# A hybrid attention layer: the softmax-times-values products as one operation per four key blocks

## The chip, the cores and the metric

The kernel runs on one core of one Trainium2 chip. The metric is the device time of one execution in microseconds. One execution was also recorded by the hardware profiler; all durations below come from it.

## The reference

One decoder layer with 1024 tokens and a model width of 1024. A normalised and modulated input is projected once; its columns belong to four groups of four heads with 64 values each: A differential, B forgetting, C stick-breaking and D sparse attention. The outputs are concatenated, projected and added to the input; a gated MLP with a short convolution follows. The change is in the last product of each attention (weights `w`, `p` or `a` times values), which the four groups share in form:

```python
def block(i):                      # 128 query rows
    ...
    p = jax.nn.softmax(s, axis=-1)
    return jnp.einsum('bhqk,bhkd->bhqd', p.astype(v.dtype), v)
```

A takes `w = p0 - lam * p1` of two softmaxes, C takes `a = exp(log_beta + tail)`. D has three such products; the selected and the window branch (at most five key blocks per query block) go through the code of the change.

## The kernel before, in words

**A program with its own scheduler.** The kernel does not issue instructions as it goes. Each helper (`mm`, `mm2`, `tr`, `copy`, `act`, `dma` and others, lines 410 to 497) records an operation through `Program.op` (line 174) with a planned length on each engine that could do it, the tiles it reads and those it writes. At the end `schedule` (line 224) plays the program through: for each engine it takes the oldest recorded operation that is ready, where ready means that its predecessors are done in the plan (plus the delays of the table `WAITS`) and that its new tiles have a slot. `issue` (line 377) then emits the instructions in that order, so the order in each engine's queue is fixed before the run; on the chip the queues go in that order and wait on semaphores. All instructions carry line 392, so groups are told apart by their tiles. One operation may hold several instructions (`mm2` holds two); nothing is placed between them.

**Slots.** The table at lines 538 to 552 gives each class of tile a quota, a group and a phase. Group `h` has 28 slots of 128 x 512 floats; a class of a later phase gets a slot only beyond the quotas of the earlier phases that are not used up. In phase 2 it holds `qst` (queries, 4), `pt` (transposed weights, 3), `ot` (output before it is transposed back, 2) and `on` (output, 2). The projections' `wr`, `wh`, `nt` and `hl` (19 in all) are phase 1. PSUM group `q` has 8 banks: four `S` (scores), two `T` (transposes), one `O` (attention output) and one `pP` (projections).

**Attention.** `attn_A`, `attn_C`, `attn_D` and `attn_B` (lines 963, 1159, 1097, 1244) run in this order. Each takes two heads at a time and query blocks of 128 rows in groups of four; block i sees n/128 = i + 1 key blocks (the window branch of D at most five). For each query block the scores go to `S`, the row minima are taken on VectorE, the exponentials on ScalarE, and the weights land in tiles `P`. Between these operations the program order mixes other matrix work: projections into `pP` beside A, C and D (`side`), the first half of the output projection beside B (`out_AC`).

**The product** is `pv_pair` (line 890), called once for each query block and head pair. For every two key blocks it transposes four 128 x 128 pieces of `P` (two blocks, two heads) into one `T` bank, copies the bank to a `pt` tile on ScalarE or VectorE (line 902), and records one `mm2` (line 419) for each key block: two matmuls that use the left and right 64 columns of TensorE for the two heads and accumulate in `O`. A matmul on 32-bit data is two records in the trace, so an `mm2` is four. `back` (line 907) copies `O` to `ot` and transposes it once the four query blocks are done. By the code there are 16 calls each in A, B and C and 32 in D, with 348 `mm2` in all; ten calls each have one, two, three and four key blocks, sixteen have five, and eight each have six, seven and eight.

Of the kernel before, what the change touches and what calls it, by code (L numbers as in the profile page):

```python
# [27 lines left out]
STEP = 1.3  # L28
EARLY = 2
DCUT = (2, 3, 3, 3)  # L30

CA_Q, CA_K, CA_V = 0, 256, 512
CB_Q, CB_K, CB_V, CB_F = 768, 1024, 1280, 1536
# [110 lines left out]
class Program:  # L144
# [274 lines left out]
    def mm2(self, outs, lhsTs, rhss, start, stop):  # L419
# [6 lines left out]
        d = max(d, 1.26 * self._mm_use(lhsTs[0], rhss[0]))  # L426
        self.op([("PE", d, f)], list(lhsTs) + list(rhss), list(outs)).share = 2.0 * self._mm_use(lhsTs[0], rhss[0]) / d

    def tr(self, out, in_, ident):
        self.op([("PE", 109.0, self._call("tensor", "transpose", (out, in_, ident), {}))], [in_, ident], [out])  # L430

# [69 lines left out]
def layer_kernel(ctx: ExitStack, tc, x, c, rel_bias, ada_w, ada_b, norm_mix_g, norm_ffn_g, w_in, w_out,  # L501
# [4 lines left out]
    K = Program(tc)  # L506
    NB, NH = 33, 28
    pool = lambda n, b, **k: ctx.enter_context(tc.tile_pool(name=n, bufs=b, **k))
    cp, bp, hp, sp = pool("cp", 1), pool("bp", 1), pool("hp", 1), pool("sp", 1)
# [7 lines left out]
    def const(shape, dt=F32, name="const"):  # L517
        ncls[0] += 1
        k = f"c{ncls[0]}_{name}"
        K.klass(k, 1, "c", 0)  # L520
        return K.tile(k, shape, dt, name)
# [12 lines left out]
    for name, quota, group, phase in (  # L534

# [7 lines left out]

# [6 lines left out]

# [2 lines left out]
        K.klass(name, quota, group, phase)  # L553
# [4 lines left out]
    def hb(cls, dt=F32):  # L558
        return K.tile(cls, (128, 512), dt)

    def ps1(cls):
        return K.tile(cls, (128, 512))


    ident = const([128, 128], name="ident")
# [324 lines left out]
    def pv_pair(P, n, vfn, dst):  # L890

        nb = n // 128
        for g0 in range(0, nb, 2):
            g1 = min(nb, g0 + 2)
            t = ps1("T")
            for j in range(g0, g1):
                for u in range(2):
                    c = 2 * (j - g0) + u
                    K.tr(t[:, c * 128:(c + 1) * 128], P[u][:, j * 128:(j + 1) * 128], ident)
            pt = hb("pt")  # L900
            w = (g1 - g0) * 256
            K.copy(pt[:, :w], t[:, :w])
            for j in range(g0, g1):
                c = 2 * (j - g0) * 128
                K.mm2([dst[0:64], dst[64:128]], vfn(j), [pt[:, c:c + 128], pt[:, c + 128:c + 256]], j == 0, j == nb - 1)

    def back(o):

# [54 lines left out]
    def attn_A(p, st):  # L963
        st, bias = st
        for i0 in (0, 4):
# [3 lines left out]
            for i in range(i0, i0 + 4):  # L969
                n = (i + 1) * 128  # L970
                Ps = []
                for u in range(2):
                    P, L = two("P", n), []
                    for m, s in enumerate(scores([[(qs[2 * u + m], st[2 * u + m][1])] for m in range(2)], i, 0, n)):
                        c = 2 * (i - i0) + u
                        l = [l0s[:, c + v:c + v + 1] for v in (0, 8)] if m == 0 else [small("l1", 1) for v in s]
                        exps(P[m], s, rows_min(s, n, bias[u]), l)
                        if len(s) > 1:
                            K.tt(l[0], l[0], l[1], OP.add)
                        L.append(l[0])  # L980
                    cf = small("cf", 1)
                    K.recip(cf, L[1])
                    K.ts(cf, cf, L[0], nlam, OP.mult, OP.mult)
                    K.stt(P[0], P[1], cf, P[0], OP.mult, OP.add)
                    Ps.append(P[0])
                pv_pair(Ps, n, VA.pair(p), o[:, (i - i0) * 128:(i - i0 + 1) * 128])
                yield i * 1.3 + STEP
# [109 lines left out]
    def attn_D(p, st):  # L1097
        qf, bias, biasC = st
        for i0 in (0, 4):
# [31 lines left out]
            for br in (1, 2):  # L1131
                o = ps1("O")
                l = small("dl", 16)
                for i in range(i0, i0 + 4):
                    k0 = 0 if br == 1 else max(0, i - 4) * 128
                    n = (i + 1) * 128 - k0
                    P = two("P", n)
                    for u, s in enumerate(scores([[(q[u], D_k[br - 1, 0]), (q[u], D_k[br - 1, 1])] for u in range(2)], i, k0, n)):
                        c = 2 * (i - i0) + u
                        exps(P[u], s, rows_min(s, n, bias[u], wmask if (br == 2 and i >= 4) else None),  # L1140
                             [l[:, c + v:c + v + 1] for v in (0, 8)])
                    pv_pair(P, n, lambda j: [VD[0][:, k0 // 128 + j, br - 1, :]] * 2, o[:, (i - i0) * 128:(i - i0 + 1) * 128])
                    yield (n / 128 - 1) * 1.3 + STEP
                f = small("df", 8)
                if i0:
                    K.tt(l[:, :8], l[:, :8], l[:, 8:], OP.add)
                K.recip(f, l[:, :8])
                K.tt(f.split(2), gates[:, i0:i0 + 4, 4 * br + 2 * p:4 * br + 2 * p + 2], f.split(2), OP.mult)
                t = on_tile()
                K.tt(t, back(o), f.bc(64), OP.mult)  # L1150
                K.tt(on, on, t, OP.add, ("POOL", "DVE"))
# [7 lines left out]
    def attn_C(p, st):  # L1159
        qf, k = st  # L1160
        for i0 in (0, 4):
            q = qf(i0)
            o = ps1("O")
            for i in range(i0, i0 + 4):
                n = (i + 1) * 128
                W = two("P", n)
                for u, z in enumerate(scores([[(q[u], k[u][0]), (q[u], k[u][1])] for u in range(2)], i, 0, n)):
                    w = W[u]
                    cs = [slice(512 * v, 512 * v + t.n) for v, t in enumerate(z)]
                    for c, t in zip(cs, z):  # L1170
                        K.act(w[:, c], t, AF.Abs)
                    K.act(w, w, AF.Exp, scale=-1.0)
                    K.act(w, w, AF.Ln, bias=1.0)
                    for c, t in zip(cs, z):
                        K.stt(w[:, c], t, 0.0, w[:, c], OP.max, OP.add)
                    K.select(w[:, n - 128:n], w[:, n - 128:n], [[-1, 128]], OP.is_gt, 0.0, 0, 1)
                    K.scan(w[:, ::-1], w[:, ::-1])
                    for c, t in zip(cs, z):
                        K.tt(w[:, c], t, w[:, c], OP.subtract)
                    K.select(w[:, n - 128:n], w[:, n - 128:n], [[-1, 128]], OP.is_gt, -BIG, 0, 1)  # L1180
                    K.act(w, w, AF.Exp)
                pv_pair(W, n, VC.pair(p), o[:, (i - i0) * 128:(i - i0 + 1) * 128])
                yield i * 1.3 + STEP
            t = on_tile()
            K.copy(t, back(o))
            o_out(2, i0, p, t)
# [471 lines left out]
    def down_mul(n, ps=None):  # L1658
# [3 lines left out]
        q0 = 0  # L1662
        for c in DCUT:
            ops = {}
# [88 lines left out]
```

## Time and profile before

| | before |
|---|---|
| median of 3 runs | 1491.72 us |
| lowest and highest run | 1485.66 and 1492.05 us |
| the profiled execution's own time | 1490.82 us |
| its span, first to last instruction | 1489.1 us |
| mean granted clock of TensorE, share of full | 0.978 |
| attention with its side work | from about 214 to 790 us of the span |

How to read the profile: PE is TensorE's matmuls, PEld its weight loads, which overlap the matmuls; DVE is VectorE, ACT ScalarE, POOL GpSimd. A group like `O<-pt,V` names the written tile and the read ones; `128*64 128x128` after it is the part of the array that is used (rows by columns) and the moving operand. Matmuls are pipelined, so the time a run of matmuls holds PE is read from its first start to the start of what follows, and the last one's own duration overlaps with what follows.

### The profile page before, as it was taken

Reading aid. Unit: us, or ns where it says so; the run is one execution under the profiler, and the core shown is the slowest. Engines: PE = TensorE matmul, PEld = TensorE weight load, DVE = VectorE, ACT = ScalarE, POOL = GpSimd, SP = SyncE. Lnnn points to the kernel's source line nnn. Section 1 sums busy time; section 2 is a strip of 40 time slices with the busy share of each in tenths; the row PEclk is TensorE's granted clock in tenths of the full one; section 3 lists DMA queues with packets and bytes.
Section 4 is the critical chain, followed back from the end, with each engine's and each line's share of the span. In section 5 each row is a group of like instructions: output and inputs, shape, how many; then the busy total and the mean of one; then the engine's idle time right before and its main releaser. Section 6 shows DMA issues by size and latency. Waiting matters only on the chain.

```text
span 1489.1 us, 24140 instructions
## 1 busy us (share of the span) xinstructions
PE 1389.8 (93%) x8573; PEld 1174.1 (79%) x8573; DVE 1120.2 (75%) x2382; ACT 703.0 (47%) x1529; POOL 217.3 (15%) x249
## 2 busy tenths in 40 slices
PE   3999999999799998999999789999999999999998
PEld 2878888888687886777877568888888888888886
DVE  7966668999779986775475886666666665898777
ACT  2531245657678655663364644334444443453342
POOL 3543310223323355100000000000000000000000
PEclk9999999999899998999999899999999999999999
DMA  9679463535431423145534322222222224963675
GB/s 353 209 213 319 134 171 93 170 91 155 114 76 49 133 92 98 41 105 162 161 105 155 113 86 86 80 83 85 85 85 80 84 85 169 370 238 99 226 248 170
DMA packets 169963, 211.24 MB, mean 142 GB/s; under 512 B 25517, under 2 KB 112214, under 8 KB 169842
## 3 DMA queue, kind: packets, MB, share of 16 engines
q1 hardware_dynamic: 168338, 208.52, 44.9%
q0 software_dynamic: 1504, 1.17, 0.5%
q8 instruction: 67, 1.10, 0.3%
q14 instruction: 54, 0.44, 0.1%
HBM read 165.30 MB, written 47.89 MB: 143 GB/s over the span
## 4 chain that ended last, share of the span: by engine, by line
PE 71%; DVE 12%; ACT 2%; issue 1%; DMA 1%; POOL 0%; SPq 0%; DVEq 0%; POOLq 0%; ACTq 0%
PE up L392 28%; PE dn L392 14%; PE pP L392 10%; PE T L392 7%; PE O L392 5%; PE S L392 4%; DVE P L392 4%; PE op L392 3%; ACT P L392 1%; DVE S L392 1%; DVE m L392 1%; DVE pt L392 1%; DVE nt L392 1%; DVE gB L392 1%; DVE hl L392 1%
## 5 line engine op out<-in xcount | busy, mean ns | idle before, releaser
L392 PE MATMUL up<-gB,fw 128*128 128x512 f32 x1320 | 303.6, 389 | 5.7 <-DVE fw L392 2.9
L392 PEld LDWEIGHTS up<-gB,fw 128*128 128x128 f32 x1320 | 247.5, 188 | 58.2 <-DVE fw L392 3.3
L392 PE MATMUL dn<-ds 128*128 128x512 f32 x924 | 209.9, 389 | 0.2 <-DVE ds L392 0.2
L392 PEld LDWEIGHTS dn<-ds 128*128 128x128 f32 x924 | 173.4, 188 | 36.6 <-DVE ds L392 0.6
L392 PE MATMUL pP<-wh,hT 128*128 128x256 f32 x1344 | 198.3, 292 | 3.4 <-DVE nt L392 1.3
L392 PEld LDWEIGHTS pP<-wh,hT 128*128 128x128 f32 x1344 | 178.7, 195 | 9.3 <-DVE nt L392 2.1
L392 ACT ACTIVATE P<-S,nm 128x512 f32<-128x512 f32 (+3 forms) x240 | 135.4, 571 | 81.9 <-DVE nm L392 63.6
L392 PE MATMUL S<-kst,qst 128*128 128x512 f32 (+2 forms) x480 | 134.0, 372 | 9.7 <-ACT P L392 5.7
L392 PE MATMUL up<-gA,fw 128*128 128x512 f32 x528 | 126.8, 395 | 7.6 <-DVE fw L392 7.6
L392 PE MATMUL T<-ident,P 128*128 128x128 f32 x696 | 113.1, 285 | 14.9 <-ACT P L392 8.9
L392 PEld LDWEIGHTS up<-gA,fw 128*128 128x128 f32 x528 | 99.8, 190 | 29.2 <-DVE fw L392 8.6
L392 PEld LDWEIGHTS T<-ident,P 128*128 128x128 f32 x696 | 79.8, 144 | 33.6 <-issue 15.1
L392 PEld LDWEIGHTS S<-kst,qst 128*128 128x128 f32 x480 | 79.1, 193 | 22.8 <-ACT P L392 9.0
L392 ACT COPY pt<-T 128x512 f32<-128x512 f32 (+1 forms) x106 | 56.5, 539 | 67.3 <-PE T L392 66.2
L392 DVE COPY pt<-T 128x512 f32<-128x512 f32 (+1 forms) x94 | 58.5, 627 | 38.6 <-PE T L392 36.1
L392 DVE TENSOR_REDUCE m<-S 128x1 f32<-128x512 f32 (+3 forms) x160 | 76.6, 488 | 7.5 <-PE S L392 6.7
L392 ACT CAST ds<-dg 128x512 fp32r<-128x512 f32 x82 | 48.2, 619 | 63.7 <-DVE dg L392 40.3
L392 DVE TENSOR_TENSOR fw<-fr,fw 128x512 fp32r<-128x512 f32 x110 | 75.1, 684 | 0.0
L392 ACT CAST fw<-fr 128x512 fp32r<-128x512 f32 x110 | 67.5, 614 | 9.6 <-DVE fw L392 9.5
L392 ACT ACTIVATE P<-P 128x256 f32<-128x256 f32 (+8 forms) x98 | 64.9, 690 | 11.5 <-POOL P L392 7.5
L392 PE MATMUL O<-pt,V 128*64 128x128 f32 x864 | 65.7, 287 | 4.2 <-DVE pt L392 2.3
L392 DVE SCALAR_TENSOR_TENSOR acc<-ada,cact,acc 128x512 f32<-128x512 f32 (+1 forms) x70 | 66.5, 950 | 3.1 <-DMA ada<-in_ada_w_dram 1.9
(295 smaller groups left out, 2323.2 us busy)
## 6 DMA issues: line engine op xcount, KB each, us to landing
dg<-d_g SPq DMA_DIRECT2D x99, 256.0 KB
fr<-in_ffn_w_up_dram SPq DMA_DIRECT2D x88, 256.0 KB
ada<-in_ada_w_dram SPq DMA_DIRECT2D x64, 256.0 KB
dg<-in_ffn_w_down_dram SPq DMA_DIRECT2D x55, 256.0 KB
d_g<-va SPq DMA_DIRECT2D x22, 512.0 KB
ada<-in_ada_w_dram SPq DMA_DIRECT2D x16, 512.0 KB
wr<-in_w_in_dram SPq DMA_DIRECT2D x32, 256.0 KB
x<-in_x_dram SPq DMA_DIRECT2D x8, 512.0 KB
```

Of the source, the lines that this page charges most:

```text
L392: return getattr(getattr(self.nc, eng), meth)(*a, **k)
```

## The change

A constant `PVB = 4` is added. `pv_pair` now goes over up to four key blocks at a time: it first records the transposes and copies of one or two `T` tiles, and then all products of these blocks and both heads as one operation `mms`, whose planned length is 0.5 x 1.03 of a matmul's use for each product plus 190 ns. The quota of `pt` goes from 3 to 4. `mm2` stays for another user.

```diff
+PVB = 4
...
+    def mms(self, prods):
+
+        fs = [self._call("tensor", "matmul", (o, a, b), dict(start=st, stop=sp)) for o, a, b, st, sp in prods]
+
+        def f():
+            return [g() for g in fs][-1]
+        d = len(prods) * 0.5 * 1.03 * self._mm_use(prods[0][1], prods[0][2]) + 190.0
+        u = len(prods) * self._mm_use(prods[0][1], prods[0][2])
+        self.op([("PE", d, f)], [x for p in prods for x in p[1:3]], [p[0] for p in prods]).share = u / d
...
-            ("qst", 4, "h", 2), ("pt", 3, "h", 2), ("ot", 2, "h", 2), ("on", 2, "h", 2),
+            ("qst", 4, "h", 2), ("pt", 4, "h", 2), ("ot", 2, "h", 2), ("on", 2, "h", 2),
...
-        for g0 in range(0, nb, 2):
-            g1 = min(nb, g0 + 2)
-            t = ps1("T")
-            for j in range(g0, g1):
-                for u in range(2):
-                    c = 2 * (j - g0) + u
-                    K.tr(t[:, c * 128:(c + 1) * 128], P[u][:, j * 128:(j + 1) * 128], ident)
-            pt = hb("pt")
-            w = (g1 - g0) * 256
-            K.copy(pt[:, :w], t[:, :w])
-            for j in range(g0, g1):
-                c = 2 * (j - g0) * 128
-                K.mm2([dst[0:64], dst[64:128]], vfn(j), [pt[:, c:c + 128], pt[:, c + 128:c + 256]], j == 0, j == nb - 1)
+        for h0 in range(0, nb, PVB):
+            h1 = min(nb, h0 + PVB)
+            pts = []
+            for g0 in range(h0, h1, 2):
+                g1 = min(h1, g0 + 2)
+                t = ps1("T")
+                for j in range(g0, g1):
+                    for u in range(2):
+                        c = 2 * (j - g0) + u
+                        K.tr(t[:, c * 128:(c + 1) * 128], P[u][:, j * 128:(j + 1) * 128], ident)
+                pt = hb("pt")
+                w = (g1 - g0) * 256
+                K.copy(pt[:, :w], t[:, :w])
+                pts += [pt[:, c:c + 128] for c in range(0, w, 128)]
+            K.mms([(dst[64 * u:64 * u + 64], vfn(j)[u], pts[2 * (j - h0) + u], j == 0, j == nb - 1)
+                   for j in range(h0, h1) for u in range(2)])
```

## Rows read from the trace of the kernel before

**Rows 1.** The page, part 1: busy us (share of the span) and instructions.

```profile
PE 1389.8 (93%) x8573; PEld 1174.1 (79%) x8573; DVE 1120.2 (75%) x2382; ACT 703.0 (47%) x1529; POOL 217.3 (15%) x249
```

**Rows 2.** Groups, 214 to 790 us, O matmuls: busy, mean ns | idle before <-releasers.

```profile
L392 PE MATMUL O<-pt,V 128*64 128x128 f32 x864 | 65.7, 287 | 4.2 <-DVE pt L392 2.3 <-ACT pt L392 1.7
...
L392 PE MATMUL O<-pt,VD 128*64 128x128 f32 x528 | 40.0, 288 | 0.1
```

**Rows 3.** Table of stretches: window, length, busy us by engine, clock, DMA, GB/s.

```profile
core 0: us, PE busy (x) PEld busy (x) DVE busy (x) ACT busy (x) POOL busy (x), PEclk, DMA share, GB/s
214.00:790.00 576.00, 532.76 (x4395) 452.15 (x4396) 454.67 (x1257) 339.40 (x882) 137.95 (x162) 0.97 0.39 111
214.00:290.00 76.00, 71.01 (x585) 62.20 (x585) 69.49 (x234) 46.37 (x143) 12.01 (x10) 0.98 0.47 134
290.00:375.00 85.00, 76.29 (x630) 67.53 (x630) 80.50 (x253) 55.67 (x165) 28.21 (x40) 0.97 0.48 127
375.00:523.00 148.00, 134.16 (x1197) 119.11 (x1196) 125.66 (x244) 104.03 (x209) 47.24 (x73) 0.96 0.34 95
523.00:600.00 77.00, 68.56 (x587) 56.09 (x585) 56.82 (x166) 41.90 (x111) 42.85 (x36) 0.93 0.33 97
600.00:690.00 90.00, 83.74 (x698) 68.21 (x699) 66.00 (x221) 51.22 (x153) 7.64 (x6) 0.96 0.27 75
690.00:790.00 100.00, 99.00 (x707) 79.01 (x706) 56.20 (x145) 40.22 (x108) 0.00 (x0) 1.00 0.48 150
```

**Rows 4.** Timeline of PE: start us, length us, what, records [idle before].

```profile
214.88 0.44 PE L392 MATMUL O<-pt,V 128*64 128x128 f32 x4 [0.42 <-DVE pt L392]
...
342.24 0.87 PE L392 MATMUL pP<-wh,hT 128*128 128x256 f32 x6
343.03 1.09 PE L392 MATMUL O<-pt,V 128*64 128x128 f32 x16
344.06 0.88 PE L392 MATMUL T<-ident,P 128*128 128x128 f32 x6
...
346.29 0.88 PE L392 MATMUL O<-pt,V 128*64 128x128 f32 x12
347.10 0.66 PE L392 MATMUL T<-ident,nt 128*128 128x128 f32 x4
...
352.91 2.66 PE L392 MATMUL pP<-wh,hT 128*128 128x256 f32 x20
355.41 0.82 PE L392 MATMUL T<-ident,P 128*128 128x128 f32 x6
...
357.90 1.09 PE L392 MATMUL T<-ident,P 128*128 128x128 f32 x8
358.75 0.94 PE L392 MATMUL S<-kst,qst 128*128 128x384 f32 x4
359.62 1.09 PE L392 MATMUL O<-pt,V 128*64 128x128 f32 x16
...
364.77 0.44 PE L392 MATMUL O<-pt,V 128*64 128x128 f32 x4
365.14 0.65 PE L392 MATMUL T<-ident,P 128*128 128x128 f32 x4
...
782.07 1.09 PE L392 MATMUL O<-pt,V 128*64 128x128 f32 x16
```

**Rows 5.** Timeline of PE from 641 us, a pair whose products run in two parts.

```profile
642.01 1.02 PE L392 MATMUL O<-pt,VD 128*64 128x128 f32 x8
642.97 1.31 PE L392 MATMUL T<-ident,P 128*128 128x128 f32 x10
644.03 0.48 PE L392 MATMUL S<-kst,qst 128*128 128x512 f32 x1
644.44 1.31 PE L392 MATMUL O<-pt,VD 128*64 128x128 f32 x20
```

**Rows 6.** Groups, 214 to 790 us, transposes and their copies (columns as in rows 2).

```profile
L392 PE MATMUL T<-ident,P 128*128 128x128 f32 x695 | 112.8, 285 | 14.9 <-ACT P L392 8.9 <-DVE P L392 2.5 <-DVE hl L392 1.7
...
L392 DVE COPY pt<-T 128x512 f32<-128x512 f32 (+1 forms) x94 | 58.5, 627 | 38.6 <-PE T L392 36.1 <-issue 1.8
L392 ACT COPY pt<-T 128x512 f32<-128x512 f32 (+1 forms) x106 | 56.5, 539 | 67.3 <-PE T L392 66.2
```

## The prediction

> **What bounds the kernel now.** I read the page first: TensorE (PE) is busy 93% of the span, VectorE (DVE) 75%, ScalarE (ACT) 47% [rows 1]. A shorter PE program could therefore shorten the whole. The weights-times-values products write the PSUM tile O; they run in a part of the span only, from 214.9 to 783 us [rows 2, 4]. So the second view is the table of stretches [rows 3]. In the 576 us from 214 to 790, PE is busy 532.8 and idle 43.2. The reader should see that DVE is nearly as full as PE in 290 to 375 (80.5 of 85 us) and in 375 to 523 (125.7 of 148), that PE's idle share is highest in 523 to 600 (8.4 of 77 us; the granted clock there is 0.93, a mean of mostly the 2.4 GHz level and partly the 1.2 GHz one), and that in 690 to 790 PE has almost no idle time (1.0 of 100). Third, the timeline of PE, which decides this case: it shows in which runs the O products stand in PE's queue [rows 4].
>
> **What the runs look like now.** By the code, 80 calls of pv_pair make 348 products of one key block for both heads. A record is half a matmul, so such a product is four records: 864 + 528 = 1392 records [rows 2]. The diff suggests short runs before, one for each transposed tile: 196 tiles, 196 runs of at most 8 records. The timeline shows something else. Going through PE's order from the first O row to the last [rows 4] and joining neighbours, I count 118 runs: 19 of 4 records, 32 of 8, 16 of 12, 40 of 16, 9 of 20 and 2 of 24. The scheduler takes the oldest ready instruction, and by the time PE is free for a pair's first product the second tile has mostly been copied too. So the run of four key blocks and both heads (16 records) is already the usual form.
>
> **Cost of a run.** From start to start in [rows 4]: the run of 4 records at 364.77 holds PE until 365.14, 0.37 us; 12 records from 346.29 to 347.10, 0.81; 16 from 343.03 to 344.06, 1.03. That is 0.055 us per record and 0.15 us fixed on leaving. On entering, six pP matmuls ahead of a run take 0.79 (342.24 to 343.03), while twenty take 2.50 (352.91 to 355.41), 0.75 for six: 0.04 more. I take 0.2 us per run. The busy time agrees: 1392 x 0.055 = 76 us, and 118 runs with the tail of a row (0.44 less 4 x 0.055, or 0.22) make 26; together 102 of the 105.7 us in [rows 2].
>
> **The change, part by part.**
> 1. *Fewer runs.* After it there are at most 120 operations of one run each: 40 pairs of one to four blocks with one, 40 pairs of five to eight with two. Neighbours can still merge, as the run of 20 at 644.44 did [rows 5]. Of the sixteen pairs with five blocks, five run in one piece now; I keep that (11 x 2 + 5 = 27), give the 24 longer pairs 48 and the short ones 40, which is 115, less the five merges across pairs that I count now: 110. So 118 becomes 110: 8 x 0.2 = 1.6 us less. The bounds: 120 runs, 0.4 us more; 80 runs, 38 x 0.2 = 7.6 us less. I take 1.6, because the order now already follows the same grouping in most pairs.
> 2. *A run waits for its second copy.* The first products could start after one tile; now the whole operation is placed after both. 16 pairs now begin with a run of two blocks and get the rest later, as at 642.01 and 644.44 [rows 5]. The price per pair lies between nothing and one copy, 0.63 us on DVE [rows 6]: 0 to 10 us. I take 0: what covers it is what stands in PE's queue between those two runs, 2.4 us from start to start filled with transposes and scores without idle. If that cover goes, the copy (0.6 us) is what is late. PE now waits for pt only 4.0 us in front of O in all [rows 2]. Behind a waiting run stand in PE's order the projections, scores and transposes of the next pair; for those exps on ACT and row minima on DVE wait.
> 3. *The fourth pt tile.* It adds no instruction and no transfer. The transposes (695 records), the 200 copies (94 on DVE and 106 on ACT) [rows 6] and every DMA stay. It lets the copies of blocks five to eight land while the first run still holds two tiles. It also takes a slot of the 28 that pt shares with qst, ot and on, so a result tile can come later. Both only move waits; 0, bounds in 4.
> 4. *Another order.* The planned lengths change. By the code one, two, three and four blocks were 269, 538, 806 and 1075 ns and become 410, 629, 849 and 1069; against the 0.37, 0.81 and 1.03 us of part one the new ones are even by 0.04, the old were short for short runs. So the scheduler will place the whole attention part somewhat differently, with the DMA issues on SP and the masks on POOL in that part as well. No row shows another order, so I bound it by stages [rows 3]: if the 576 us had the idle share of 214 to 290 (5.0 of 76, 6.6%), idle would be 38, 5 us less; with that of 523 to 600 (10.9%) it would be 63, 20 us more. I take 0, as the present total is nearer to the lower end, and keep both ends.
> 5. *pv_pair's other work* keeps its kind and count; the final output, out projection and the gated MLP from 790 us on are untouched.
>
> Sum: -1.6 us on the profiled execution's 1490.8 (span 1489.1 and 1.7 around it), so 1489.2. The median of the three runs, 1491.7, stands 0.9 above it: 1490.
>
> **A rule weighed.** The timeline shows 0.15 to 0.2 us lost at each run's ends. The Trainium skill, page TensorEngine Tiling (Array Packing), section Tiling Modes, says that changing the tiling mode drains TensorE, and O runs on 128 by 64 tiles between 128 by 128 work, so the trace agrees. Taken with the diff alone it would promise the gain of the first rival. The same page, section Performance Considerations, speaks against a gain: tiling does not speed the PSUM eviction, which may become the limit; by it the sum would be 0. Here the eviction is unchanged, 115 us on two engines [rows 6], and DVE's share bears that out in 290 to 523 but not after 690 [rows 3].
>
> **Rivals.**
> *A, face value: the runs fall by as many as the tiles suggest.* 196 - 120 = 76 runs less at 0.2 = 15 us: 1476. For it: the loss per run is plain, and PE is nearly full. Against it: the timeline has 118 runs, not 196. Only a merging to about 80 (-7.6) with less idle time besides would get near. Chance 0.08.
> *B, the pipeline closes up.* With the first run placed later and a tile more, the transposes of blocks five and six go in front of the first run, and their copies pass behind it. Now both groups of transposes follow that run (8 records at 357.90, the next run at 359.62) [rows 4]. It would take half of PE's idle in 375 to 600 (13.8 + 8.4 = 22.3 us): -11, and -1.6 from runs: 1478. For it: those pairs wait now. Against it: PE is filled by pP meanwhile, and DVE at 85% and more of 290 to 523 would be the next limit. Chance 0.16.
> *C, slower: the second copy is waited for.* In the stretch from 523 to 690 PE has little other work to lay in between, and the 16 pairs that start after one tile must wait for four more transposes (0.43 us: eight start at 357.90 and the next work at 358.75 [rows 4]) and a copy (0.63 us): 16 x 1.06 = 17 us, 1508 with the 0.9 above. It decides as soon as PE has less than about 1 us of other ready work at that point. For it: clock 0.93 and 11% idle there. Against it: 0.1 us of idle in front of those O records now [rows 2]. Chance 0.15.
> *The forecast, no change that can be told:* 0.61.
>
> **How the numbers follow.** About 0.5%, 7.5 us, is what a measurement of this kernel can tell from no change; its three runs spread over 6.4. A and B are faster by more, 0.24; the forecast is the same, 0.61; C is slower, 0.15. The range: below, the forecast's own ends (-1.6 - 5 - 4) and B give 1478; above, part 2's whole bound of 10 us gives 1500. A's and most of C's chance lie outside.
>
> **What would show it.** Right: the O runs number 105 to 120 with the 16-record run still the commonest; PE's busy time on O falls by about 2 us from 105.7; PE's idle from 214 to 790 stays within 38 to 50 us; DVE and ACT copies unchanged in sum. A would show fewer than 90 runs and O at 95 us. B would show transposes ahead of the first run in pairs of five to eight blocks, and less idle from 375 to 600. C would show PE waiting for pt in front of O for 10 us or more. The forecast is wrong if the idle moves by over 8 us either way, above all if the granted clock in 523 to 600 leaves 0.93, or if stages after 790 change, which nothing here touches.

## The result, and the profile after

The changed kernel takes 1479.67 us (median of five runs, 1476.49 to 1481.05) against 1491.72 before: ratio 0.9932, interval 0.991 to 0.9954, so 10 us less, with 7 to 13 as bounds (the two medians alone are 12 apart). The time lies inside the range of the prediction, but beyond the 0.5% that it called no change; that outcome had a chance of 0.24.

The profiled execution after took 1479.34 us with a span of 1477.6, 11.5 us less than the profiled one of before. The page after, part 1 (answers to [rows 1]):

```profile
PE 1382.1 (94%) x8573; PEld 1172.4 (79%) x8573; DVE 1119.3 (76%) x2380; ACT 700.1 (47%) x1525; POOL 228.4 (15%) x255
```

PE has the same number of records and 7.7 us less busy time. The O groups from 214 to 790 us (answers to [rows 2]), and the transposes and copies (to [rows 6]):

```profile
L393 PE MATMUL T<-ident,P 128*128 128x128 f32 x695 | 112.7, 284 | 12.7 <-ACT P L393 7.1 <-DVE P L393 3.5 <-ACT qk_y L393 0.8
...
L393 PE MATMUL O<-pt,V 128*64 128x128 f32 x864 | 64.7, 289 | 4.3 <-DVE pt L393 4.2
...
L393 DVE COPY pt<-T 128x512 f32<-128x512 f32 (+1 forms) x97 | 59.8, 624 | 29.0 <-PE T L393 27.9 <-issue 0.2 <-DMA kst<-d_bk 0.2
L393 ACT COPY pt<-T 128x512 f32<-128x512 f32 (+1 forms) x103 | 55.0, 540 | 59.6 <-PE T L393 56.6 <-PE S L393 1.8
...
L393 PE MATMUL O<-pt,VD 128*64 128x128 f32 x528 | 36.2, 280 | 0.0
```

O holds PE for 100.9 us in place of 105.7, the copies for 114.8 in place of 115.0, and PE waits for pt in front of O as long as before (4.2 us against 4.0). In PE's order I count 99 runs of O in place of 118: pairs of up to four blocks have one run each, 15 of 16 pairs with five blocks have one, and in D even six, seven and eight blocks join.

Where did the time go? The first and last starts of O by its value tile (VD is D's), before and after, date the stages:

```profile
L392 PE MATMUL O<-pt,V x864: 272/273/476, 214.9 to 782.9; 128*64 128x128 f32 x173
L392 PE MATMUL O<-pt,VD x528: 272/273/476, 523.5 to 673.3; 128*64 128x128 f32 x176
```

```profile
L393 PE MATMUL O<-pt,V x864: 272/273/477, 215.7 to 771.9; 128*64 128x128 f32 x173
L393 PE MATMUL O<-pt,VD x528: 272/273/477, 523.6 to 662.0; 128*64 128x128 f32 x176
```

A and C end where they ended: D's first product starts at 523.5 and 523.6 us. From the last O start to the end it is nearly equal too (706.2 and 705.7 us). In this pair of traces nearly the whole gain lies in D, whose products end 11.3 us earlier. The table of stretches for D's two head pairs, the first cut at the first O of the second pair and the second at the first O of B, before and after (columns as in [rows 3]):

```profile
523.50:615.60 92.10, 80.78 (x669) 66.44 (x668) 69.71 (x218) 52.34 (x146) 45.09 (x37) 0.93 0.31 90
615.60:675.40 59.80, 56.42 (x521) 46.13 (x520) 44.53 (x149) 35.46 (x103) 3.61 (x3) 0.97 0.26 66
```

```profile
523.60:605.80 82.20, 75.25 (x662) 64.43 (x661) 68.23 (x211) 53.09 (x149) 46.01 (x39) 0.95 0.34 101
605.80:664.10 58.30, 54.05 (x519) 45.45 (x519) 42.23 (x143) 35.40 (x103) 3.60 (x3) 0.98 0.27 68
```

The first pair of heads in D takes 82.2 us in place of 92.1: PE is busy 5.5 us less and idle 4.4 us less. Of the busy time there, O has 2.8 us less (18.21 against 21.04, in 17 runs in place of 26), and the projections pP have 1.7 us less, because ten of their records (79 against 89) now stand outside this pair. Before, PE had there a stretch in which it stood (timeline of PE before, and below it the table row of the end of that stretch):

```profile
571.55 1.09 PE L392 MATMUL O<-pt,VD 128*64 128x128 f32 x16
...
576.85 1.75 PE L392 MATMUL S<-kst,qst 128*128 128x512 f32 x6 [0.95 <-ACT P L392]
579.47 0.66 PE L392 MATMUL T<-ident,ot 128*128 128x128 f32 x4 [0.86 <-ACT P L392]
...
581.62 0.80 PE L392 MATMUL S<-kst,qst 128*128 128x512 f32 x1 [1.27 <-ACT P L392]
585.95 1.24 PE L392 MATMUL T<-ident,nt 128*128 128x128 f32 x4 [3.53 <-DVE nt L392]
...
589.63 1.98 PE L392 MATMUL O<-pt,VD 128*64 128x128 f32 x16
```

```profile
581.40:591.60 10.20, 6.35 (x32) 4.78 (x33) 9.27 (x20) 5.03 (x16) 4.85 (x3) 0.50 0.20 62
```

No O run starts between 571.55 and 589.63, PE is idle 6.6 of these 18 us, and the run at 589.63 takes 1.98 us for 16 records, not 1.09: after these waits the granted clock is 0.50, the 1.2 GHz level, from 581.4 to 591.6 us. The last transposes of the key projection (T<-ident,nt) stand at the head of PE's queue and wait 3.5 us for DVE. After, the same place looks so:

```profile
572.15 1.09 PE L393 MATMUL O<-pt,VD 128*64 128x128 f32 x16
...
574.80 1.09 PE L393 MATMUL O<-pt,VD 128*64 128x128 f32 x16
575.82 0.66 PE L393 MATMUL T<-ident,nt 128*128 128x128 f32 x4
...
579.97 1.31 PE L393 MATMUL O<-pt,VD 128*64 128x128 f32 x20
```

The transposes of nt don't wait, and the next run follows after 5 us. This left two theories. **Runs:** fewer runs of O give the gain. **Order:** the scheduler found another order, and the gain is the stall in D that this order happens not to have.

### The profile page after: what moved, and what is told of

Read it like the earlier page. It is cut to its first block, busy times and chain, and to the rows that moved or that the text cites. A ratio compares the mean times of both kernels' runs of the same rounds, so it can differ in the third digit from the quotient of the medians.

```text
span 1477.6 us, 24130 instructions
## 1 busy us (share of the span) xinstructions
PE 1382.1 (94%) x8573; PEld 1172.4 (79%) x8573; DVE 1119.3 (76%) x2380; ACT 700.1 (47%) x1525; POOL 228.4 (15%) x255
## 4 chain that ended last, share of the span: by engine, by line
PE 68%; DVE 13%; issue 2%; ACT 2%; POOL 1%; DMA 0%; SPq 0%; POOLq 0%; DVEq 0%; ACTq 0%
PE up L393 28%; PE dn L393 14%; PE pP L393 9%; PE T L393 6%; DVE P L393 5%; PE O L393 4%; PE S L393 4%; PE op L393 3%; DVE m L393 1%; DVE S L393 1%; DVE pt L393 1%; ACT P L393 1%; DVE nt L393 1%; DVE gB L393 1%; DVE on L393 0%
## 5 line engine op out<-in xcount | busy, mean ns | idle before, releaser
L393 PE MATMUL S<-kst,qst 128*128 128x512 f32 (+3 forms) x480 | 132.8, 369 | 7.9 <-DVE P L393 3.1
L393 PEld LDWEIGHTS T<-ident,P 128*128 128x128 f32 x696 | 81.0, 144 | 31.4 <-ACT P L393 11.3
L393 DVE TENSOR_REDUCE m<-S 128x1 f32<-128x256 f32 (+3 forms) x160 | 76.2, 488 | 4.6 <-PE S L393 4.0
L393 ACT ACTIVATE P<-P 128x128 f32<-128x128 f32 (+8 forms) x98 | 64.0, 690 | 20.3 <-POOL P L393 16.5
```

Of the source, the lines that this page charges most:

```text
L393: return getattr(getattr(self.nc, eng), meth)(*a, **k)
```

## The experiments

All ratios are against the kernel before, measured beside each kernel on the same chip (medians of before 1488.9 to 1490.3 us).

**The price of a run, by cutting (a_cut).** The planned order of after stays; only the last key block's products of a run are issued one PE operation later, where nothing in between uses their tiles.

```diff
+            if o.i in self.cut:
+                for g in self.parts[o.i][:-2]:
+                    o.inst = g()
+            else:
+                o.inst = f()
+            for p in self.after.get(o.i, []):
+                for g in self.parts[p][-2:]:
+                    g()
```

> Kernel after in its own planned order, except that 72 of its runs are cut: the last key block's products of the run come one PE operation later. Theory 'runs', if 0.6 us per run explains the whole gain: 43 us more. At 0.2 to 0.25 us per run as the timeline prices it: 14 to 18 us more if PE is the limit throughout, less where it waits anyway. Theory 'order': 5 to 18 us more, and D still ends about 10 us earlier than before.

Measured: 1495.27 us, ratio 1.0037 (1.0022 to 1.0051). The trace has 168 runs, 69 more than after. Against the kernel with three pt tiles, measured beside it (1479.61, below; it has after's order on PE), this is 15.7 us more, 0.23 us per run. Its O groups:

```profile
L402 PE MATMUL O<-pt,V 128*64 128x128 f32 x864 | 75.4, 292 | 4.2 <-DVE pt L402 3.9
...
L402 PE MATMUL O<-pt,VD 128*64 128x128 f32 x528 | 40.0, 283 | 0.5 <-DVE pt L402 0.5
```

PE is busy on O 115.4 us in place of 100.9: 14.5 us for 69 runs. So a run that is added to this order has a price that reaches the end whole. If 19 fewer runs give back the same price each, they are worth 4.4 us, less than half of what the change gave; 0.6 us per run is excluded. D ends 5.7 us earlier than before (last O start 667.7 against 673.3), not the 10 expected, but its first pair still takes 83.5 us, with 27 runs there against before's 26:

```profile
524.10:607.60 83.50, 75.82 (x662) 62.65 (x661) 65.77 (x211) 52.91 (x149) 46.03 (x39) 0.99 0.33 99
```

So it is not the number of runs that decides between 92 and 82 us in that pair.

**Fewer runs in the old order (b_joined).** The planned order of before stays, but the products of a pair's group of up to four blocks are held until the last of the group.

```diff
+        for g in K.pv:
+            last = max(at[i] for i in g)
+            for i in sorted(g, reverse=True):
...
+                moves[i] = last
```

> Kernel before with its own planned order, except that a pair's products of up to four key blocks are held back until the last of them, so that they run together: 105 runs of O in place of 118, every other instruction in the same order. Theory 'runs' (the gain of the change comes from fewer runs): if 19 fewer runs gave all 11.5 us, 13 fewer give 8 us less; at 0.2 to 0.25 us per run, as the timeline prices one, 3 us less. Theory 'order' (the gain comes from the other order in D, which has no stall at 576 to 590 us): the stall stays and the time falls by 0 to 3 us.

Measured: 1490.39, ratio 1.0007 (0.9993 to 1.002), with 105 runs. O holds PE for less, but nothing is gained:

```profile
L393 PE MATMUL O<-pt,V 128*64 128x128 f32 x864 | 65.9, 289 | 3.5 <-DVE pt L393 2.2 <-ACT pt L393 1.2
...
L393 PE MATMUL O<-pt,VD 128*64 128x128 f32 x528 | 38.0, 285 | 0.1
```

```profile
522.60:613.50 90.90, 79.24 (x671) 66.20 (x670) 70.52 (x218) 52.14 (x147) 45.08 (x37) 0.93 0.32 91
```

The 1.8 us saved on O (103.9 against 105.7) do not show in the time, and D's first pair still takes 90.9 us. The interval reaches from 1 us less to 3 more, so it leaves out the 3 us that 13 runs would give back at a_cut's price. 'Runs' alone does not carry the gain, and the price of an added run is not simply returned by a removed one.

**Three pt tiles (a_pt3).**

```diff
-            ("qst", 4, "h", 2), ("pt", 4, "h", 2), ("ot", 2, "h", 2), ("on", 2, "h", 2),
+            ("qst", 4, "h", 2), ("pt", 3, "h", 2), ("ot", 2, "h", 2), ("on", 2, "h", 2),
```

> Kernel after with three pt tiles instead of four. The planned order is the same on PE, DVE, ACT and POOL; one load changes places with its neighbours on SP. Both theories: within 2 us of after, so the fourth tile has no part in the gain.

Measured: 1479.61, ratio 0.9934 (0.9918 to 0.9951), the same as the whole change. In this order the fourth tile does nothing.

**The stall itself (b_wo_late, b_wo_shift).** On DVE the multiplications ahead of the waiting transposes were slow. Timelines of DVE and of POOL before:

```profile
580.72 0.16 DVE L392 TENSOR_TENSOR qk_t<-qk_t,qk_y 128x8 f32<-128x8 f32 x1
580.92 0.17 DVE L392 TENSOR_SCALAR qk_t<-qk_t 128x8 f32<-128x8 f32 x1
581.34 2.00 DVE L392 TENSOR_TENSOR qk_y<-qk_y,qk_t 128x8 f32<-128x8 f32 x1
...
583.53 2.70 DVE L392 TENSOR_TENSOR nt<-nt,qk_y 128x256 f32<-128x256 f32 x2
```

```profile
580.97 2.35 POOL L392 TENSOR_TENSOR wo<-wor,wo 128x1024 fp32r<-128x1024 f32 x1 [3.52 <-ACT wo L392]
583.28 2.34 POOL L392 TENSOR_TENSOR wor<-wor,gta 128x1024 f32<-128x1024 f32 x1
```

A multiplication of eight columns took 2.00 us (0.16 for the one at 580.72) and ended, at 583.34, with POOL's subtraction at 583.32. The Trainium skill, page SBUF — State Buffer, section SBUF: two separate sides, says that DVE and GpSimd share one pair of ports, held for a whole instruction, when the DVE operation reads two SBUF inputs and the GpSimd operation reads SBUF; the rows agree. The two kernels keep before's order and move POOL's later work on the output weights away. In both, the first of the two POOL operations, the subtraction, stays beside the small multiplication.

```diff
+    held = [o for o in done[last - 40:last + 1] if wo(o)]
+    done = done[:last - 40] + [o for o in done[last - 40:last + 1] if not wo(o)] + held + done[last + 1:]
```

> Kernel before in its own planned order, except that three operations of the output projection's weights (two on POOL, one load on SP) go behind the last key projection's normalisation instead of beside it; the O runs stay at 118. Theory 'order': the two DVE multiplications of nt, 2.7 us for two, fall to about 1.2, the wait of PE's transposes of nt (3.5 us) falls under 1.5, and the time falls by 2 to 8 us, more than the wait if the clock drop at 581 us goes as well. Theory 'runs': within 1 us of before.

Measured: 1496.87, ratio 1.0053 (1.0033 to 1.0074): slower. The two multiplications of nt fell from 2.70 to 0.75 us, the small one still took 2.00. The wait for nt fell to 1.87 us, but a worse one came:

```profile
583.31 1.24 PE L392 MATMUL T<-ident,nt 128*128 128x128 f32 x4 [1.87 <-DVE nt L392]
...
595.59 0.70 PE L392 MATMUL O<-pt,VD 128*64 128x128 f32 x4 [5.88 <-ACT pt L392]
```

```profile
594.23 1.04 ACT L392 CAST wo<-wor 128x1024 fp32r<-128x1024 f32 x1 [6.92 <-POOL wor L392]
595.17 0.85 ACT L392 COPY pt<-T 128x256 f32<-128x256 f32 x2
```

My edit had left the cast of the next weight where it was in ACT's queue; it waited for POOL, and a pt copy stood behind it. The second kernel shifts the whole rest of the chain.

```diff
+    shift = {o.i: n + 60.5 for n, o in enumerate(done) if n >= last - 40 and wo(o)}
+    done = [o for _, o in sorted(((shift.get(o.i, n), o) for n, o in enumerate(done)), key=lambda z: z[0])]
```

> Kernel before in its planned order, with the last nine operations of the output projection's weights (loads, POOL and ACT) all shifted later by about 60 places, so that neither POOL runs beside the last key normalisation nor ACT waits for a late weight. Theory 'order': PE's wait for nt falls from 3.5 to under 2 us and no new wait of 5.9 us appears; 2 to 6 us less than before. If the loss there has another cause, within 1.5 us of before.

Measured: 1490.87, ratio 1.0006 (0.9989 to 1.0023). The late cast is gone and the wait for nt is 1.58 us; the small multiplication still takes 1.99 us, because the subtraction on POOL (578.22 to 580.57 us) was not moved. D's first pair takes 90.2 us:

```profile
578.60 1.99 DVE L392 TENSOR_TENSOR qk_y<-qk_y,qk_t 128x8 f32<-128x8 f32 x1
```

```profile
520.80:611.00 90.20, 81.48 (x671) 67.09 (x670) 67.83 (x218) 52.27 (x146) 45.18 (x37) 0.92 0.31 92
```

So 1.95 of the 3.53 us of this wait went, D's first pair got 1.9 us shorter in the trace, and the time as a whole did not fall. A kernel without any of the wait was not tried. The wait marks the bad place but is not the whole of it; the waits for P ahead of it and the lower clock behind it stayed.

**The change in parts (d_only, abc_only).** One part of the pairs keeps the loop of before under the name `pv_old`.

```diff
-                pv_pair(P, n, VB.pair(p), o[:, (i - i0) * 128:(i - i0 + 1) * 128])
+                pv_old(P, n, VB.pair(p), o[:, (i - i0) * 128:(i - i0 + 1) * 128])
```

> The change in D alone; A, B and C keep the products of two blocks at a time. Theory 'order': the whole gain was found in the first head pair of D, so this gives 8 to 12 us less than before, with A and C as before. Theory 'runs' (after the joined kernel hardly tenable): a share of the gain by its share of the runs saved, about half, 5 to 6 us.

> The change in A, B and C alone; D keeps two blocks at a time. Theory 'order', if D keeps the order of before: within 3 us of before, with the stall of about 18 us between two runs of D at 571 to 590. Theory 'runs': about half the gain, 5 to 6 us less. A third: D is planned anew because what stands before it differs, and then anything between -12 and +6 us, to be read from whether the stall is there.

Measured: D alone 1485.02, ratio 0.9974 (0.9957 to 0.9991); A, B and C alone 1484.4, ratio 0.9959 (0.9937 to 0.9981). Each has 107 runs. The two add up to the whole (0.26% and 0.41% against 0.68%). D alone gives 4 us, not the 8 to 12 that 'order' expected. And in both traces D's first pair takes about 85 us, 84.9 and 85.8 by the starts of O: even the kernel that leaves D's code alone has the stall no more. This fits the third expectation, a new plan, and not 'order' as I had put it.

**Other orders of the same work.** If the order decides, then a small change of a planned length must move the time though the work stays the same.

```diff
-        d = max(d, 1.26 * self._mm_use(lhsTs[0], rhss[0]))
+        d = max(d, 1.27 * self._mm_use(lhsTs[0], rhss[0]))
```

> Kernel before, with only the planned length of a two-head product raised by 1% (factor 1.27 in place of 1.26): nothing of the work differs, only the order the scheduler finds; 119 runs of O. Theory 'order': the time may move by several us either way, 3 to 12, and part of the gain can come with no change of the products at all. Theory 'runs': within 2 us of before.

> Kernel before, with the planned length of a product lowered by 1% (factor 1.25): another planned order, 122 runs. Theory 'grouping': within 4 us of before. Theory 'luck of the order': 5 to 12 us less is possible. With the variant raised by 1% it gives the spread that the order alone makes.

> Kernel after, with 180 in place of 190 ns in the planned length: the same work in another planned order, 98 runs. Theory 'grouping': within 4 us of after. Theory 'luck of the order': as far from after as from before, 5 to 12 us slower than after.

> Kernel after, with 200 in place of 190 ns: the same work in another planned order, 97 runs. The same expectations as with 180; if both lie within 4 us of after, the gain belongs to the grouping and not to one order.

> Kernel after, with the run's planned length by the formula of before (269 ns for each two-head product, nothing fixed): 99 runs. Theory 'grouping' (one operation per four blocks brings the gain, fewer runs at 0.23 us and later placed products): 6 to 12 us less than before, as after. Theory 'lengths' (the better planned length brings it): within 4 us of before. Theory 'luck of the order': anywhere from 12 us less to 3 more.

| kernel | runs of O | ratio to before (interval) |
|---|---|---|
| before, 1.26 | 118 | 1 |
| b_len127 | 119 | 1.0011 (0.9992 to 1.003) |
| b_len125 | 122 | 1.0065 (1.0042 to 1.0088) |
| after, 190 ns | 99 | 0.9932 (0.991 to 0.9954) |
| a_len180 | 98 | 0.9941 (0.9923 to 0.9959) |
| a_len200 | 97 | 1.0004 (0.9987 to 1.002) |
| a_oldlen | 99 | 1.0016 (0.9999 to 1.0033) |

Ten nanoseconds in a planned length take the whole gain away (a_len200), and so does the old formula (a_oldlen). In a_len200 it goes in D's first pair again:

```profile
526.60:618.60 92.00, 77.11 (x660) 65.98 (x659) 71.72 (x208) 51.65 (x142) 46.98 (x38) 0.93 0.30 90
```

```profile
579.39 2.83 PE L393 MATMUL O<-pt,VD 128*64 128x128 f32 x24 [4.29 <-DVE pt L393]
```

```profile
571.83 3.36 DVE L393 TENSOR_TENSOR qk_t<-ss,qk_y 128x8 f32<-128x8 f32 x1
...
575.83 2.90 DVE L393 TENSOR_TENSOR nt<-nt,qk_y 128x256 f32<-128x256 f32 x2
578.66 0.68 DVE L393 COPY pt<-T 128x512 f32<-128x512 f32 x1
```

```profile
572.78 2.38 POOL L393 TENSOR_TENSOR wo<-wor,wo 128x1024 fp32r<-128x1024 f32 x1
575.86 2.59 POOL L393 TENSOR_TENSOR wor<-wor,gta 128x1024 f32<-128x1024 f32 x1 [0.70 <-DMA wor<-in_w_out_dram]
```

Here the run itself waits for a pt copy, which stands on DVE behind the normalisation, and that runs beside POOL's operations. In a_oldlen D's first pair is good (81.2 us), and C and the rest behind the attention are 8 us longer each than in after (159.1 and 705.7 us):

```profile
363.20:530.30 167.10, 143.35 (x1250) 127.05 (x1249) 144.14 (x271) 109.65 (x224) 58.07 (x85) 0.93 0.33 93
...
778.80:1492.20 713.40, 691.49 (x3061) 569.34 (x3055) 515.30 (x819) 296.38 (x495) 0.00 (x0) 0.99 0.42 138
```

The loss in a_oldlen is also what theory 'lengths' expected; a_len200, whose lengths differ from after's by 10 ns only, speaks against it as the whole cause. Of the products-apart orders, b_len127 moved less than 'order' asked, and b_len125 got 10 us slower, which no theory had. Yet in b_len127 D's first pair is good with no product grouped:

```profile
529.60:615.40 85.80, 75.45 (x660) 62.75 (x659) 69.22 (x213) 53.03 (x147) 44.96 (x36) 0.98 0.33 96
```

The 6 us won there are lost elsewhere: its first O starts 3.5 us later, and C takes 163.3 us in place of 158.7. By the starts of O, D's first pair takes 81 to 82 us in after, a_len180 and a_oldlen, 85 to 86 in d_only, abc_only and b_len127, and 90 to 92 in before, b_len125 and a_len200. In the last three the granted clock in this pair is 0.92 or 0.93, in the six others 0.94 to 0.98; no run separates the lower clock from the waits that come with it.

The mean of the four orders with one operation per four blocks is 0.9973, of the three with products apart 1.0025: 0.5% or 8 us between them. Each group spreads over 10 to 13 us and the two overlap, so seven orders don't tell how much the grouping gives in the mean. By a_cut's price about 4 us of the measured 10 would belong to the runs and the rest to the order that this version met. That split is argued, not shown: in b_joined the price did not come back.

## Why the prediction was right or wrong

- *What bounds it, and the runs that already stood there:* right. The run of 16 records is still the commonest (37 of 99), and the change removed 19 runs, not the 76 that the diff suggests. Rival A fell with that.
- *Part 1, fewer runs:* right in kind, too small in size. I kept eleven of sixteen five-block pairs in two runs and all longer ones; 15 of 16 joined, and five longer ones in D. So 99 in place of 110. The price of 0.2 us was 0.23 by cutting. By that price the term is 4.4 us, not 1.6, within its bound of 7.6 (O's own busy time fell by 4.8); b_joined shows that such a saving need not reach the end.
- *Part 2, waiting for the second copy:* the 0 held in this order (PE waits 4.2 us for pt in front of O, 4.0 before). In the joined kernel, which holds products back in the old order, the saving of 1.8 us on O did not show, and in a_len200 one such wait alone was 4.29 us. Rival C is real as a mechanism, but it is set by the order and not by the operation.
- *Part 3, the fourth tile:* right, nothing in this order.
- *Part 4, another order:* the step that failed in size. I took 0 between 5 less and 20 more from the idle shares of stages. By subtraction it gave about 6 less here; the orders measured span 10 us with products apart and 13 with products grouped. The bounds counted idle time alone; D's first pair lost PE busy time too, 5.5 us of 9.9: fewer runs of O, projections that moved out of the pair, and less work at the 1.2 GHz level (PE is busy 9.75 us in stretches at 0.50 before, 6.8 after; an estimate from the 1.98 us against 1.09 of a 16-record run makes that about 1.3 us).
- *Rival B* came near in time (1478) and half in mechanism: transposes of the fifth block and beyond do pass ahead of the run, which is how the runs joined. But A and C, where it should have acted as well, ended where they had ended, and PE's idle time from 375 to 600 us fell by 5 us (22.3 to 17.3), not by 11.
- *The signs it named:* several came out against it. The runs number 99, below 105, and O's busy time fell by 4.8 us, not 2. The granted clock from 523 to 600 us left 0.93 for 0.98, which it had called a sign of a wrong forecast; PE's idle time from 214 to 790 moved by 4.7 us, to 38.5, inside the bounds it gave.
- *The range:* that the time lies inside it is partly luck. Its low end, 1478, came from Rival B and from a sum whose last term, 4 us, is worked out nowhere in the prediction; neither is what happened. With 10 ns more in a planned length the same operation takes 1491.7 us (a_len200), about the 1490 forecast.
- *Stages after 790 us:* untouched in after, as said; in a_oldlen the part behind the attention moved by 8 us.

What stays open is which placement in D's first pair decides, and how much of the gain belongs to the grouping. Cutting the wait for nt from 3.53 to 1.58 us returned at most 2 of the 10 us, and no kernel was tried that keeps before's order everywhere but there.

## What to carry to other kernels

Before pricing a regrouping, count in the timeline how the queue already stands: here the scheduler had made most of the long runs itself. Where a planner sets the order, run a few neighbours of its constants beside every change: here a planned length of 200 in place of 190 ns moved the time by as much as the change did, so a single gain of half a per cent says little of the idea behind it. And a stall in one queue is often the shadow of another engine's placement: moving POOL's work away shortened one wait and made a longer one on ACT.

## What the runs showed of the hardware that was not expected

A DVE multiplication of two SBUF tensors with eight columns, 0.16 us a little earlier in the same chain, took 2.00 us beside a POOL operation of 2.35 us, and in a_len200 3.36 us, ending at 575.19 with a POOL operation that ended at 575.16. It is not only operations with two inputs: in a_len180 a TENSOR_SCALAR of eight columns, which reads one tensor, took 2.70 us and ended at 571.04, where a POOL operation ended at 571.00. In a_cut a switch between the 128 by 64 products and other PE work cost 0.23 us both ways together, and PE's trace shows nearly all of it as busy time (0.21 us per run), not as idle time.
